# An encoder layer on one core: the start addresses of the moving token tiles, and the order of a chunk's first matmuls

## The chip, the cores and the metric

The kernel runs on one core of one Trainium2 chip. The metric is the device time of one execution in microseconds. Engines are named as the profile names them: PE is the matrix engine, PEld its loading of stationary operands, DVE the vector engine, ACT the scalar engine, POOL GpSimd and SP the engine whose queue issues the weight loads.

## The reference

One layer works on 256 tokens of 2048 channels in float32. Cut to what matters here (`h` is the normalised input):

```python
z = h @ w_in                                   # 2048 -> 13312 columns
conv_b, conv_c, conv_in, q, k, v, g_a, g_b = split(z)
y_a = (conv_b * conv3(conv_c * conv_in)) @ w_out_conv
y_b = block_gqa(rope(rmsnorm(q)), rope(rmsnorm(k)), v) @ w_out_attn
mixed = (sigmoid(g_a + ba) * y_a + sigmoid(g_b + bb) * y_b) @ w_merge
x = x + rmsnorm(mixed, norm_mix_post)
f = square(relu(rmsnorm(x, norm_mlp_pre) @ w_up)) @ w_down
x = x + rmsnorm(f, norm_mlp_post)
```

## The kernel before

All products are done in chunks of 512 weight columns over a contraction of 2048, cut into 16 tiles of 128. Every operand is split into a high part and a low remainder (`split`), so that one product takes three matmuls: high by high, high by low, low by high. Weights come as granules of two contraction tiles: a 128x1024 transfer into `raw`, a cast on ACT into `whi` and a subtraction on DVE into `wlo`.

A chunk is computed in one of two functions.

- `linear_channels` (lines 182, 186 and 189) keeps the weights stationary, 128 columns at a time, and streams the 256 tokens past them. For each granule a loop over the four groups of 128 output channels (`c`) calls `step(c, ...)`, which does both contraction tiles of the granule, three matmuls each. A call therefore has 4 x 16 x 3 = 192 matmuls of 256 columns. The last two granules are done pair by pair of channel groups.
- `linear` (lines 152 to 154) keeps the tokens stationary and streams 512 weight columns past them: 2 x 16 x 3 = 96 matmuls of 512 columns.

In the order of the program: three `linear` calls on `hT` for K, V and the first Q; then, for each of four heads' groups, three `linear_channels` calls on `hT` for the convolution branch with the attention of the group between them (transposes on lines 231 and 419, scores and values on lines 386 to 388), and a `linear` call on `hT` for the next Q; then 16 `linear_channels` calls for gates and branch outputs (`hT` and `yT` by turns, then `hT` and `oT`); four `linear` calls on `mT` for the merge; one `linear` and three `linear_channels` calls on `x2T` for the first quarter of the MLP's up projection; four `linear` calls on `fT` (down projection); and three times four `linear_channels` calls on `x2T` and four `linear` calls on `fT`. `later` and `tick` put the attention's steps at fixed places between the granules, so the order on PE is written out by hand.

The token operands live in three large buffers with the tags A, B and C (`pair`). `LATE` shifts a buffer's data by some floats. What counts below is an **offset**: the start of the moving operand less the start of the stationary one in the same partition, modulo 256 bytes. In the built program all `raw`, `whi` and `wlo` tiles begin at 192 modulo 256. `hT` (tag A, 48 floats late), `yT`, `oT` and `x2T` begin at 128, `mT` and `fT` at 192, K and V (`kv`) at 128, queries and probabilities (`qh`, `ql`, `ph`, `pl`) at 192. Each contraction tile, each half of tokens and each group of channels is a multiple of 256 bytes long, so an operand's offset is the same in all its matmuls:

- `linear_channels`: 128 - 192, which is -64 (192 modulo 256)
- `linear` on `hT` and `x2T`: 192 - 128 = +64
- `linear` on `mT` and `fT`: 0
- scores -64, values +64

Of the kernel before, what the change touches and what calls it, by code (L numbers as in the profile page):

```python
# [9 lines left out]
F32 = mybir.dt.float32  # L10
F32R = mybir.dt.float32r
# [4 lines left out]
P = 128  # L16
D = 2048
T = 256
NT = T // P
KT = D // P  # L20
CH = 512
# [11 lines left out]
def trunk_kernel(  # L33
# [27 lines left out]
    const = ctx.enter_context(tc.tile_pool(name="const", bufs=1))  # L61

    sm = ctx.enter_context(tc.tile_pool(name="sm", bufs=2))
    wts = ctx.enter_context(tc.tile_pool(name="wts", bufs=WB))
    big = ctx.enter_context(tc.tile_pool(name="big", bufs=1))
    wk = ctx.enter_context(tc.tile_pool(name="wk", bufs=2))
    ps_acc = ctx.enter_context(tc.tile_pool(name="ps_acc", bufs=4, space=bass.MemoryType.PSUM))
# [17 lines left out]

    LATE = {"A": {True: 48, False: 0}, "B": {True: 0, False: 16}, "C": {True: 0}}

    def pair(tag, moving):

        n, at = 2 * KT * T, LATE[tag][moving]  # L90
        flat = big.tile([P, n + max(LATE[tag].values())], F32R, tag=tag, name=tag)
        both = flat[:, at : at + n].rearrange("p (h k t) -> p h k t", h=2, k=KT)
        return both[:, 0], both[:, 1]

# [7 lines left out]
    def later(delay, fn):  # L102
        todo.append((clock[0] + 2 * delay, fn))
# [36 lines left out]
    def linear(act, wv, done, k0=0, k1=KT, lag=0, ahead=None):  # L140

        ah, al = act
        accs = [ps_acc.tile([P, CH], F32, name="acc") for _ in range(NT)]

        def step(t, k, wh, wl):
            ts_ = slice(t * P, (t + 1) * P)
            for g in range(KG):
                a = k - k0 + g  # L150
                first, last = a == 0, a == k1 - k0 - 1
                nc.tensor.matmul(accs[t], lhsT=ah[:, a, ts_], rhs=wh[:, g, :], start=first, stop=False)  # L152
                nc.tensor.matmul(accs[t], lhsT=ah[:, a, ts_], rhs=wl[:, g, :], start=False, stop=False)  # L153
                nc.tensor.matmul(accs[t], lhsT=al[:, a, ts_], rhs=wh[:, g, :], start=False, stop=last)  # L154
# [12 lines left out]

    def linear_channels(act, wv, done):

        ah, al = act
        accs = [ps_acc.tile([P, 2, T], F32, name="acc") for _ in range(CH // P // 2)]

        def step(c, k, wh, wl):
            cs = slice(c * P, (c + 1) * P)
            acc = accs[c // 2][:, c % 2, :]
            for g in range(KG):
                a = k + g  # L180

                nc.tensor.matmul(  # L182
                    acc, lhsT=wh[:, g, cs], rhs=ah[:, a, :], start=a == 0 and c % 2 == 0, stop=False,
                    skip_group_check=True,
                )
                nc.tensor.matmul(  # L186
                    acc, lhsT=wh[:, g, cs], rhs=al[:, a, :], start=False, stop=False, skip_group_check=True
                )
                nc.tensor.matmul(  # L189
                    acc, lhsT=wl[:, g, cs], rhs=ah[:, a, :], start=False, stop=a == KT - 1, skip_group_check=True  # L190
                )
# [85 lines left out]

    hT = pair("A", True)

    def first_operands(k, n):  # L280
        xt = mx.tile([P, KA, T], F32, tag="rope", bufs=4, name="xt")
        nc.sync.dma_start(xt[:, :n, :], xT[:, k : k + n, :])
        for i in range(n):
            split(xt[:, i, :], hT[0][:, k + i, :], hT[1][:, k + i, :], scale=g_pre[:, k + i : k + i + 1])

# [95 lines left out]

    oT = pair("C", True)
    yT = pair("B", True)

# [5 lines left out]
    def attention(j):  # L390
# [41 lines left out]
        def heads_out(hp, ovs):  # L432
            h0 = j * GRP + hp
            split(ovs[0], oT[0][:, h0 : h0 + 2, :], oT[1][:, h0 : h0 + 2, :])

# [11 lines left out]
    def conv(j):  # L447
# [29 lines left out]
        def outer(c, acc):  # L477
            b = wk.tile([P, 2, T], F32, tag="cc", bufs=CCB, name="cc")
            with tc.high_priority():
                nc.vector.tensor_tensor(b, acc, cv[:, c : c + 2, :], op=ALU.mult)  # L480
            d = j * 4 + c
            later(2 + c // 2, lambda: split(b, yT[0][:, d : d + 2, :], yT[1][:, d : d + 2, :]))

# [32 lines left out]
    for j in range(4):  # L516
# [6 lines left out]
        linear_channels(yT, w_oc[j], done)  # L523
    mT = pair("B", False)
    for j in range(4):
        g = gate(C_GB, j, 1)
        def done(c, acc):
            y = wk.tile([P, 2, T], F32, tag="cc", bufs=CCB, name="cc")
            with tc.high_priority():
                nc.vector.tensor_tensor(y, acc, g[:, c : c + 2, :], op=ALU.mult)  # L530
            d = j * 4 + c
            nc.vector.tensor_tensor(y, y, m[:, d : d + 2, :], op=ALU.add)
            split(y, mT[0][:, d : d + 2, :], mT[1][:, d : d + 2, :])

        linear_channels(oT, w_oa[j], done)
# [16 lines left out]
    ss1 = ss01[:, 1]  # L552
    ss2 = const.tile([P, NT, 4], F32, name="ss2")
# [20 lines left out]
    def residual(t, x2):  # L574
        r = row_rsqrt(ss1, t, t)
        ts_ = slice(t * P, (t + 1) * P)
        for c in range(4):
# [9 lines left out]
            nc.vector.tensor_tensor(n, tr, g_mlp[:, ds].unsqueeze(2).broadcast_to([P, 4, P]), op=ALU.mult)  # L587
            split(n, x2T[0][:, ds, ts_], x2T[1][:, ds, ts_])

# [15 lines left out]
    facc = big.tile([P, 2, NT, D], F32, tag="B", name="facc")[:, 0]  # L605
    ss3 = const.tile([P, NT, 4], F32, name="ss3")
    outv = out.rearrange("(t p) d -> p t d", p=P)

    def hidden_channels(q, j, fT):


        def done(c, acc):
# [4 lines left out]
            d = j * 4 + c  # L617
            split(f, fT[0][:, d : d + 2, :], fT[1][:, d : d + 2, :])

        linear_channels(x2T, w_up[q * 4 + j], done)  # L620

    def hidden(q, j, fT):
# [9 lines left out]
        def sink(c, tr):  # L632
            d = j * 4 + c
            split(tr, fT[0][:, d : d + 2, :], fT[1][:, d : d + 2, :])

# [43 lines left out]
    for q in range(4):  # L679
        fT = pair("A", False)  # L680
        for j in range(4):
# [67 lines left out]
```

## Time and profile before

| | |
|---|---|
| median of 3 runs | 1602.23 us (1602.12 to 1602.23) |
| the profiled execution | 1602.84 us, span 1601.1 us |
| granted PE clock, mean | 0.999 |
| PE busy | 1589.0 us, 99% of the span |
| PEld busy | 1482.2 us |
| DVE busy, ACT busy | 947.5 us, 710.7 us |
| read from HBM | 302.44 MB, 190 GB/s over the span |

Every line of the profile that speaks of time in the program counts from the first instruction (the span). The profiled execution took 1.7 us more than its span, and 0.6 us more than the median of the runs. PE's busy time is of little use for single matmuls: the profile models a matmul's end, and matmuls overlap. How fast they follow each other is read as the length of a stretch over the number of matmuls that the loops put into it; a stretch's own count also takes in the one or two matmuls still draining at its start.

### The profile page before, as it was taken

The numbers are of one execution on the slowest core, as the hardware profiler recorded it, in microseconds if no ns is written. First come the engines' busy times: TensorE is split into PE (matmuls) and PEld (weight loads), VectorE is DVE, ScalarE is ACT, GpSimd is POOL, SyncE is SP. The second block draws the span as 40 slices with busy tenths as digits, with TensorE's granted clock in tenths as the row PEclk, the third lists the DMA queues.
The fourth block names the chain that finished last, engine by engine and source line by source line (L and its number), as shares of the span: only waits on it lengthen the run. The fifth ranks groups of instructions, "written<-read, shape, count | busy, mean of one in ns | idle before, by whom it ended". The sixth has DMA issues, their size and how long they took to land.

```text
span 1601.1 us, 26865 instructions
## 1 busy us (share of the span) xinstructions
PE 1589.0 (99%) x11210; PEld 1482.2 (93%) x11210; DVE 947.5 (59%) x1107; ACT 710.7 (44%) x860; POOL 35.6 (2%) x23
## 2 busy tenths in 40 slices
PE   9999999999999999999999999999999999999997
PEld 7899999999999999999988898899988998899986
DVE  6767676677765455555555865445655555555654
ACT  7444444444454444444444644434433343333441
POOL 0110101001000000000000000000000000000000
PEclk9999999999999999999999999999999999999999
DMA  8655545555476655666764665655555555556562
GB/s 324 200 176 165 184 148 186 183 174 183 159 248 193 193 192 189 201 195 195 251 206 150 216 192 190 195 188 186 191 191 194 185 189 192 194 184 191 189 206 84
DMA packets 86297, 306.28 MB, mean 191 GB/s; under 512 B 9632, under 2 KB 10016, under 8 KB 85920
## 3 DMA queue, kind: packets, MB, share of 16 engines
q1 hardware_dynamic: 84608, 300.32, 57.8%
q10 hardware_dynamic: 1568, 4.25, 0.8%
q8 instruction: 87, 1.43, 0.4%
q14 instruction: 34, 0.28, 0.1%
HBM read 302.44 MB, written 2.10 MB: 190 GB/s over the span
## 4 chain that ended last, share of the span: by engine, by line
PE 98%; DVE 1%; DMA 0%; POOL 0%; issue 0%; ACT 0%; SPq 0%; DVEq 0%; POOLq 0%; ACTq 0%
PE acc L182 20%; PE acc L186 20%; PE acc L189 20%; PE acc L153 12%; PE acc L154 12%; PE acc L152 12%; PE at L388 0%; PE at L387 0%; PE at L386 0%; PE tr L419 0%; DMA raw<-in_w_in 0%; PE tr L231 0%; POOL rs L243 0%; DVE wlo L77 0%; PE tr L584 0%
## 5 line engine op out<-in xcount | busy, mean ns | idle before, releaser
L77 DVE TENSOR_TENSOR wlo<-raw,whi 128x1024 fp32r<-128x1024 f32 (+1 forms) x561 | 684.3, 1222 | 578.2 <-ACT whi L76 576.3
L76 ACT CAST whi<-raw 128x1024 fp32r<-128x1024 f32 (+1 forms) x561 | 588.5, 1050 | 751.7 <-PE acc L186 380.3
L182 PE MATMUL acc<-A,whi 128*128 128x256 f32 x1280 | 357.2, 279 | 0.0
L189 PE MATMUL acc<-A,wlo 128*128 128x256 f32 x1280 | 355.2, 277 | 0.0
L186 PE MATMUL acc<-A,whi 128*128 128x256 f32 x1280 | 355.2, 277 | 0.0
L182 PE MATMUL acc<-C,whi 128*128 128x256 f32 x1216 | 340.5, 280 | 0.0
L189 PE MATMUL acc<-C,wlo 128*128 128x256 f32 x1216 | 340.3, 280 | 0.0
L186 PE MATMUL acc<-C,whi 128*128 128x256 f32 x1216 | 340.3, 280 | 0.0
L153 PE MATMUL acc<-wlo,A 128*128 128x512 f32 x704 | 275.0, 391 | 1.0 <-DVE wlo L77 1.0
L152 PE MATMUL acc<-whi,A 128*128 128x512 f32 x704 | 274.4, 391 | 1.2 <-ACT whi L76 1.2
L154 PE MATMUL acc<-whi,A 128*128 128x512 f32 x704 | 274.8, 390 | 0.0
L182 PEld LDWEIGHTS acc<-A,whi 128*128 128x128 f32 x1280 | 241.6, 189 | 0.2
L186 PEld LDWEIGHTS acc<-A,whi 128*128 128x128 f32 x1280 | 240.4, 188 | 0.2
L189 PEld LDWEIGHTS acc<-A,wlo 128*128 128x128 f32 x1280 | 240.4, 188 | 0.0
L189 PEld LDWEIGHTS acc<-C,wlo 128*128 128x128 f32 x1216 | 231.5, 190 | 0.0
L182 PEld LDWEIGHTS acc<-C,whi 128*128 128x128 f32 x1216 | 229.0, 188 | 0.2
L186 PEld LDWEIGHTS acc<-C,whi 128*128 128x128 f32 x1216 | 228.2, 188 | 0.2
L153 PEld LDWEIGHTS acc<-wlo,A 128*128 128x128 f32 x704 | 132.3, 188 | 30.3 <-DVE wlo L77 2.6
L152 PEld LDWEIGHTS acc<-whi,A 128*128 128x128 f32 x704 | 132.2, 188 | 29.6 <-ACT whi L76 2.1
L154 PEld LDWEIGHTS acc<-whi,A 128*128 128x128 f32 x704 | 132.3, 188 | 27.4
L182 PE MATMUL acc<-B,whi 128*128 128x256 f32 x256 | 70.7, 276 | 0.0
L186 PE MATMUL acc<-B,whi 128*128 128x256 f32 x256 | 70.7, 276 | 0.0
(144 smaller groups left out, 1112.7 us busy)
## 6 DMA issues: line engine op xcount, KB each, us to landing
raw<-in_w_in SPq DMA_DIRECT2D x207, 512.0 KB, 4.4
raw<-in_w_up SPq DMA_DIRECT2D x128, 512.0 KB, 3.8
raw<-in_w_dn SPq DMA_DIRECT2D x128, 512.0 KB, 3.4
raw<-in_w_oc SPq DMA_DIRECT2D x32, 512.0 KB, 4.4
raw<-in_w_oa SPq DMA_DIRECT2D x32, 512.0 KB, 4.3
raw<-in_w_mg SPq DMA_DIRECT2D x32, 512.0 KB, 4.3
xj<-in_x SPq DMA_DIRECT2D x4, 512.0 KB, 8.3
xr<-in_x ACTq DMA_DIRECT2D x1, 2048.0 KB, 10.0
```

The lines of the kernel that those rows point to most:

```text
L76: nc.scalar.copy(hi, src)
L77: nc.vector.tensor_tensor(lo, src, hi.bitcast(F32), op=ALU.subtract)
L152: nc.tensor.matmul(accs[t], lhsT=ah[:, a, ts_], rhs=wh[:, g, :], start=first, stop=False)
L153: nc.tensor.matmul(accs[t], lhsT=ah[:, a, ts_], rhs=wl[:, g, :], start=False, stop=False)
L154: nc.tensor.matmul(accs[t], lhsT=al[:, a, ts_], rhs=wh[:, g, :], start=False, stop=last)
L182: nc.tensor.matmul(acc, lhsT=wh[:, g, cs], rhs=ah[:, a, :], start=a == 0 and c % 2 == 0, stop=False, skip_group_check=True,)
L186: nc.tensor.matmul(acc, lhsT=wh[:, g, cs], rhs=al[:, a, :], start=False, stop=False, skip_group_check=True)
L189: nc.tensor.matmul(acc, lhsT=wl[:, g, cs], rhs=ah[:, a, :], start=False, stop=a == KT - 1, skip_group_check=True)
```

## The change

Tag A's buffer now holds `hT` as two pieces: its first contraction tile, high and low, at the start of the buffer, and the other fifteen behind it, 16 floats (64 bytes) on. Tag C's buffer holds `oT` and `x2T` the other way round, with the first contraction tile behind the rest. `yT` keeps its tiles together, 64 bytes on. `mT` and `fT` begin at the buffer's start as before. The pool of small tiles is taken after the large ones, which moves the addresses a little, and two small tiles of sums are shared instead of new.

In the built program the weights still begin at 192 modulo 256. The first tile of `hT`, `oT` and `x2T` begins at 192 too, the other fifteen and all of `yT` at 0, `mT` and `fT` at 192, `kv` at 192. So the offsets become:

- `linear_channels` on `hT`, `oT`, `x2T`: 0 in the first contraction tile, +64 in the other fifteen; on `yT`: +64 in all
- `linear` on `hT` and `x2T`: 0 in the first tile, -64 in the other fifteen
- `linear` on `mT` and `fT`: 0 as before
- scores and values: 0

In `linear_channels` the first granule's loops are turned: the first contraction tile is done for all four channel groups, then the second. `fill` splits a block that holds the first tile in two, one piece for each place.

```diff
-    def pair(tag, moving):
-        n, at = 2 * KT * T, LATE[tag][moving]
-        flat = big.tile([P, n + max(LATE[tag].values())], F32R, tag=tag, name=tag)
...
+    GAP = 16
...
+        def __init__(self, tag, moving=False, first=False, last=False):
+            n = 2 * KT * T
+            pad = 3 * GAP if last else GAP
+            flat = big.tile([P, n + pad], F32R, tag=tag, name=tag)
+            self.first = None
+            if first or last:
+                at, rest = (0, 2 * T + GAP) if first else (n - 2 * T + pad, 0)
+                self.first = flat[:, at : at + 2 * T].rearrange("p (h k t) -> p h k t", h=2, k=1)
+                n -= 2 * T
+            else:
+                rest = GAP if moving else 0
+            self.rest = flat[:, rest : rest + n].rearrange("p (h k t) -> p h k t", h=2, k=n // (2 * T))
...
+        def fill(self, k, src, ts_=slice(None)):
+
+            for at, n, hi, lo in self.parts(k, src.shape[1], ts_):
+                split(src[:, at : at + n, :], hi, lo)
...
-                for c in range(CH // P):
-                    step(c, *gran)
+
+                for gs in [[g] for g in range(KG)] if gran[0] == 0 else [range(KG)]:
+                    for c in range(CH // P):
+                        step(c, *gran, gs)
...
-    hT = pair("A", True)
+    hT = Operand("A", first=True)
+    oT = Operand("C", last=True)
...
-    yT = pair("B", True)
+    yT = Operand("B", moving=True)
...
-    mT = pair("B", False)
+    mT = Operand("B")
...
-    x2T = pair("C", True)
+    x2T = Operand("C", last=True)
...
-        fT = pair("A", False)
+        fT = Operand("A")
```

On PE, in the first granule of an up call (`x2T` is C, and the call's two accumulators `acc` hold two channel groups each), these rows of before are the second contraction tile of the second channel group and the first of the third:

```order
L182 MATMUL acc_11145<-C_8882,whi_11149 128x256
L186 MATMUL acc_11145<-C_8882,whi_11149 128x256
L189 MATMUL acc_11145<-C_8882,wlo_11150 128x256
L182 MATMUL acc_11146<-C_8882,whi_11149 128x256
L186 MATMUL acc_11146<-C_8882,whi_11149 128x256
L189 MATMUL acc_11146<-C_8882,wlo_11150 128x256
```

After the change the fourth to fifteenth matmul of the same call are these; the first nine of the rows are the first tile of groups 2, 3 and 4, the last three the second tile of group 1.

```order
L213 MATMUL acc_11149<-C_8883,whi_11153 128x256
L217 MATMUL acc_11149<-C_8883,whi_11153 128x256
L220 MATMUL acc_11149<-C_8883,wlo_11154 128x256
L213 MATMUL acc_11150<-C_8883,whi_11153 128x256
L217 MATMUL acc_11150<-C_8883,whi_11153 128x256
L220 MATMUL acc_11150<-C_8883,wlo_11154 128x256
L213 MATMUL acc_11150<-C_8883,whi_11153 128x256
L217 MATMUL acc_11150<-C_8883,whi_11153 128x256
L220 MATMUL acc_11150<-C_8883,wlo_11154 128x256
L213 MATMUL acc_11149<-C_8883,whi_11153 128x256
L217 MATMUL acc_11149<-C_8883,whi_11153 128x256
L220 MATMUL acc_11149<-C_8883,wlo_11154 128x256
```

The second accumulator is now first written after six matmuls of the call instead of twelve; the number of matmuls and the weights they read are the same. All 12 matmuls of offset 0 stand together at the call's start.

On ACT, while the merge's result is turned into `x2T` (`cc` holds four contraction tiles of it), before:

```order
L76 CAST whi_9646<-raw_9644 128x1024
L76 CAST C_8882<-cc_9478 128x4x128
L76 CAST C_8882<-cc_9488 128x4x128
L76 CAST whi_9664<-raw_9662 128x1024
L76 CAST C_8882<-cc_9498 128x4x128
```

and after:

```order
L75 CAST whi_9650<-raw_9648 128x1024
L75 CAST C_8883<-cc_9479 128x128
L75 CAST C_8883<-cc_9479 128x3x128
L75 CAST C_8883<-cc_9491 128x4x128
L75 CAST whi_9668<-raw_9666 128x1024
L75 CAST C_8883<-cc_9501 128x4x128
```

The cast of the block that holds the first tile has become two. DVE's subtraction is split likewise. This happens three times in the program: once for `oT` and once for each half of the tokens of `x2T`.

## Rows read from the trace of the kernel before

**Rows 1.** The page: busy time, share and instructions by engine.
```profile
PE 1589.0 (99%) x11210; PEld 1482.2 (93%) x11210; DVE 947.5 (59%) x1107; ACT 710.7 (44%) x860; POOL 35.6 (2%) x23
```

**Rows 2.** All waits of PE: us in total, times, longest us.
```profile
PE acc L152 <- ACT whi L76: 1.2, 2, 0.8
PE tr L263 <- DVE half L270: 1.1, 1, 1.1
PE acc L153 <- DVE wlo L77: 1.0, 2, 0.5
PE tr L584 <- DVE mg L579: 0.4, 1, 0.4
```

**Rows 3.** Stages: us; busy (count) PE PEld DVE ACT POOL; clock, DMA share, GB/s.
```profile
76.91:442.09 365.18, 365.18 (x2882) 353.35 (x2881) 254.27 (x374) 171.24 (x238) 22.55 (x8) 1.00 0.54 173
442.09:790.19 348.10, 348.10 (x3074) 348.10 (x3073) 189.17 (x179) 157.08 (x173) 0.00 (x0) 1.00 0.64 207
904.49:972.94 68.45, 68.45 (x586) 68.44 (x584) 42.47 (x45) 30.87 (x34) 0.00 (x0) 1.00 0.66 216
972.94:1060.02 87.08, 87.08 (x386) 72.08 (x385) 42.44 (x37) 38.23 (x41) 0.00 (x0) 1.00 0.60 193
1060.02:1150.48 90.46, 90.46 (x770) 90.45 (x768) 50.41 (x52) 37.09 (x40) 0.00 (x0) 1.00 0.59 187
```

**Rows 4.** PE groups by form, 442.09 to 790.19 us: busy us, mean ns of one.
```profile
L182 PE MATMUL acc<-A,whi 128*128 128x256 f32 x512 | 141.3, 276 | 0.0
...
L182 PE MATMUL acc<-C,whi 128*128 128x256 f32 x256 | 70.7, 276 | 0.0
```

**Rows 5.** PE groups by form, 1060.02 to 1150.48 us.
```profile
L182 PE MATMUL acc<-C,whi 128*128 128x256 f32 x256 | 71.9, 281 | 0.0
```

**Rows 6.** PE groups by form, 76.91 to 442.09 us.
```profile
L189 PE MATMUL acc<-A,wlo 128*128 128x256 f32 x768 | 213.9, 278 | 0.0
...
L387 PE MATMUL at<-kv,qh 128*128 128x256 f32 x32 | 9.0, 281 | 0.0
```

**Rows 7.** PE groups by form, 99.82 to 112.53 us.
```profile
L186 PE MATMUL acc<-A,whi 128*128 128x256 f32 x33 | 9.3, 281 | 0.0
```

**Rows 8.** PE's timeline, four transposes: start us, us, engine, line, names, count.
```profile
93.72 0.60 PE L231 MATMUL tr<-ident,ra 128*128 128x128 f32 x4
```

**Rows 9.** PE groups by form, 91.68 to 93.71 us.
```profile
L182 PE MATMUL acc<-A,whi 128*128 128x256 f32 x6 | 1.7, 276 | 0.0
```

**Rows 10.** PE groups by form, 94.28 to 99.80 us.
```profile
L186 PE MATMUL acc<-A,whi 128*128 128x256 f32 x16 | 4.5, 281 | 0.0
```

**Rows 11.** Single stretches: us, PE busy (count), clock, DMA share, GB/s.
```profile
904.49:909.95 5.46, 5.46 (x49) 1.00 0.93 287
972.94:975.02 2.08, 2.08 (x11) 1.00 0.09 14
994.74:1016.49 21.75, 21.75 (x97) 1.00 0.59 194
248.49:270.47 21.98, 21.98 (x99) 1.00 0.62 192
30.43:36.03 5.60, 5.60 (x26) 1.00 1.01 398
```

**Rows 12.** Values, PE groups by form, 115.72 to 116.25 us.
```profile
L386 PE MATMUL at<-ph,kv 128*128 128x256 f32 x2 | 0.6, 277 | 0.0
```

**Rows 13.** Values, PE groups by form, 119.7 to 120.3 us.
```profile
L386 PE MATMUL at<-ph,kv 128*128 128x256 f32 x2 | 0.6, 280 | 0.0
```

**Rows 14.** The page: the weights' split on DVE and ACT.
```profile
L77 DVE TENSOR_TENSOR wlo<-raw,whi 128x1024 fp32r<-128x1024 f32 (+1 forms) x561 | 684.3, 1222 | 578.2 <-ACT whi L76 576.3
L76 ACT CAST whi<-raw 128x1024 fp32r<-128x1024 f32 (+1 forms) x561 | 588.5, 1050 | 751.7 <-PE acc L186 380.3
```

**Rows 15.** Groups of ACT and of DVE, 880 to 905 us: the split of `x2T`.
```profile
L76 ACT CAST C<-cc 128x512 fp32r<-128x512 f32 x5 | 3.0, 619 | 4.3 <-DVE cc L587 4.3
L77 DVE TENSOR_TENSOR C<-cc,C 128x512 fp32r<-128x512 f32 x5 | 3.3, 685 | 0.0
```

More of the change, by code (lines that the diff above doesn't have):

```diff
@@ L82, in split, with __call__, parts @@
             )
-    LATE = {"A": {True: 48, False: 0}, "B": {True: 0, False: 16}, "C": {True: 0}}
-    def pair(tag, moving):
-        n, at = 2 * KT * T, LATE[tag][moving]
-        flat = big.tile([P, n + max(LATE[tag].values())], F32R, tag=tag, name=tag)
-        both = flat[:, at : at + n].rearrange("p (h k t) -> p h k t", h=2, k=KT)
-        return both[:, 0], both[:, 1]
+    GAP = 16
+    class Operand:
+        def __init__(self, tag, moving=False, first=False, last=False):
[10 more added lines that the diff above has]
+            self.rest = flat[:, rest : rest + n].rearrange("p (h k t) -> p h k t", h=2, k=n // (2 * T))
+        def __call__(self, k, ts_=slice(None)):
+            _, _, hi, lo = self.parts(k, 1, ts_)[0]
+            return hi[:, 0, :], lo[:, 0, :]
+        def parts(self, k, n, ts_=slice(None)):
+            if self.first is None:
+                return [(0, n, self.rest[:, 0, k : k + n, ts_], self.rest[:, 1, k : k + n, ts_])]
+            out = []
+            if k == 0:
+                out.append((0, 1, self.first[:, 0, :, ts_], self.first[:, 1, :, ts_]))
+            lo = max(k, 1)
+            if k + n > lo:
+                ks = slice(lo - 1, k + n - 1)
+                out.append((lo - k, k + n - lo, self.rest[:, 0, ks, ts_], self.rest[:, 1, ks, ts_]))
+            return out
+        def fill(self, k, src, ts_=slice(None)):
+            for at, n, hi, lo in self.parts(k, src.shape[1], ts_):
+                split(src[:, at : at + n, :], hi, lo)
     todo = []
@@ L151, in step @@
                 first, last = a == 0, a == k1 - k0 - 1
-                nc.tensor.matmul(accs[t], lhsT=ah[:, a, ts_], rhs=wh[:, g, :], start=first, stop=False)
-                nc.tensor.matmul(accs[t], lhsT=ah[:, a, ts_], rhs=wl[:, g, :], start=False, stop=False)
-                nc.tensor.matmul(accs[t], lhsT=al[:, a, ts_], rhs=wh[:, g, :], start=False, stop=last)
+                ah, al = act(a, ts_)
+                nc.tensor.matmul(accs[t], lhsT=ah, rhs=wh[:, g, :], start=first, stop=False)
+                nc.tensor.matmul(accs[t], lhsT=ah, rhs=wl[:, g, :], start=False, stop=False)
+                nc.tensor.matmul(accs[t], lhsT=al, rhs=wh[:, g, :], start=False, stop=last)
             if k + KG == k1:
@@ L168, in linear_channels, with step @@
     def linear_channels(act, wv, done):
-        ah, al = act
         accs = [ps_acc.tile([P, 2, T], F32, name="acc") for _ in range(CH // P // 2)]
-        def step(c, k, wh, wl):
+        def step(c, k, wh, wl, gs=range(KG)):
             cs = slice(c * P, (c + 1) * P)
             acc = accs[c // 2][:, c % 2, :]
-            for g in range(KG):
+            for g in gs:
                 a = k + g
+                ah, al = act(a)
                 nc.tensor.matmul(
-                    acc, lhsT=wh[:, g, cs], rhs=ah[:, a, :], start=a == 0 and c % 2 == 0, stop=False,
+                    acc, lhsT=wh[:, g, cs], rhs=ah, start=a == 0 and c % 2 == 0, stop=False,
                     skip_group_check=True,
@@ L283, in first_operands @@
         for i in range(n):
[L284 removed]
+            split(xt[:, i, :], *hT(k + i), scale=g_pre[:, k + i : k + i + 1])
     norm_row = wk.tile([P, 2, T], F32, name="bias", bufs=1)
@@ L433, in heads_out @@
             h0 = j * GRP + hp
-            split(ovs[0], oT[0][:, h0 : h0 + 2, :], oT[1][:, h0 : h0 + 2, :])
+            oT.fill(h0, ovs[0])
         at = 9
@@ L481, in outer @@
             d = j * 4 + c
-            later(2 + c // 2, lambda: split(b, yT[0][:, d : d + 2, :], yT[1][:, d : d + 2, :]))
+            later(2 + c // 2, lambda: yT.fill(d, b))
         linear_channels(hT, w_in[C_CC + j], first)
@@ L532, in done @@
             nc.vector.tensor_tensor(y, y, m[:, d : d + 2, :], op=ALU.add)
-            split(y, mT[0][:, d : d + 2, :], mT[1][:, d : d + 2, :])
+            mT.fill(d, y)
         linear_channels(oT, w_oa[j], done)
@@ L587, in residual @@
             nc.vector.tensor_tensor(n, tr, g_mlp[:, ds].unsqueeze(2).broadcast_to([P, 4, P]), op=ALU.mult)
-            split(n, x2T[0][:, ds, ts_], x2T[1][:, ds, ts_])
+            x2T.fill(c * 4, n, ts_)
     for j in range(4):
@@ L605, in trunk_kernel @@
     facc = big.tile([P, 2, NT, D], F32, tag="B", name="facc")[:, 0]
-    ss3 = const.tile([P, NT, 4], F32, name="ss3")
+    ss3 = ss01[:, 1]
     outv = out.rearrange("(t p) d -> p t d", p=P)
@@ L617, in done @@
             d = j * 4 + c
-            split(f, fT[0][:, d : d + 2, :], fT[1][:, d : d + 2, :])
+            fT.fill(d, f)
         linear_channels(x2T, w_up[q * 4 + j], done)
@@ L633, in sink @@
             d = j * 4 + c
-            split(tr, fT[0][:, d : d + 2, :], fT[1][:, d : d + 2, :])
+            fT.fill(d, tr)
         linear(x2T, w_up[q * 4 + j], done, lag=LAG if q == 0 and j == 0 else 0)
```

10 lines of the change are left out of this document (4 added, 6 removed).

## The prediction, made before the changed kernel ran

> **What bounds the kernel now.** I read the page first: PE is busy for 1589.0 of the 1601.1 us, DVE for 59% and ACT for 44% [rows 1]. The list of PE's waits is nearly empty: 3.7 us in all, none over 1.1 us [rows 2]. So the time is the number of matmuls times the distance between them, and I cut the span into stages at the first matmul of each [rows 3]. The loops say how many matmuls a stage has, and the quotient is the distance. The gate and branch stage has 16 calls of 192: 348.10 us / 3072 = 113.31 ns. An up stage of the MLP has 4 calls of 192: 90.46 us / 768 = 117.79 ns (two more up stages are 90.46 us as well). Same form, same granted clock of 1.00, that is the upper of the clock's two levels, 2.4 GHz; 4.47 ns of difference.
>
> The groups by form say the same without counting. In the gate stage a channel matmul lasts 276 ns in the mean, whichever buffer its tokens come from [rows 4]; in the up stage it lasts 281 ns [rows 5]. Tag C stands in both, at the same address with the same offset of -64 to the same weight buffers. So at this offset there are **two levels that each hold themselves**, and what went before decides between them. I call them fast (276 ns long, 113.31 apart) and slow (281 and 117.79).
>
> What tips them? Inside a call, four transposes do [rows 8]: 276 ns ahead of them [rows 9], 281 behind them and to the call's end [rows 10]. Slow is then handed on: the next call stays slow for its first 96 matmuls [rows 7]. At a call's start it depends on the chunk before. Behind `linear` at offset +64 the first up call ran 48 matmuls in 5.46 us, fast [rows 11]. Behind `linear` at offset 0 the up stages are slow throughout [rows 3, 5]. `linear` has levels of its own: at offset 0 96 matmuls take 21.75 us, 226.6 ns each, exactly twice the fast distance; at +64 they take 229.0 ns in a Q call (21.98 us) and 233.3 ns in the V call (24 in 5.60 us) [rows 11].
>
> The attention stage is mixed: 278 ns in the mean [rows 6], two fifths of the way from 276 to 281, so about 40% of its 2304 channel matmuls are slow.
>
> **The change, part by part.** It removes no matmul and adds none. Each term is a number of matmuls times a distance.
>
> Up projection. If each call begins fast and stays so, three stages give 3 x 768 x 4.47 ns = 10.3 us. In the first quarter the 48 fast matmuls leave 528, at 117.79 ns 62.2 of the 63.0 us that follow (the rest is eight transposes); they give 528 x 4.47 = 2.4 us. Together **-12.7 us**.
>
> Attention. The transposes inside calls stay, and will tip the level again. What a fresh start of each call can take away is slowness handed on: 96 matmuls in each of four head groups [rows 7], 384 x 4.47 = **-1.7 us**. Bounds: -4.1 us if none is slow any more (40% of 2304), +6.2 us if all are.
>
> Scores and values go to offset 0. The 96 score matmuls last 281 ns now [rows 6]; the 96 values 277 behind a fast call and 280 behind a slow one [rows 12, 13]. Between nothing and 0.6 us is to be had; I take half, **-0.3 us**.
>
> The first tile at offset 0. 39 calls have it (20 on `hT`, 4 on `oT`, 15 on `x2T`), 468 matmuls. No channel matmul of before runs at offset 0. The nearest row is `linear` at offset 0, which costs nothing over its fast distance [rows 11]; from above I bound it by `linear`'s worst, 6.7 ns, thus 3.1 us. I take **+1.0 us**, near the lower end, for two changes of offset in every call.
>
> `linear` on `hT` and `x2T` at -64. No `linear` of before runs there. Between 226.6 and 233.3 ns per matmul it is worth from -2.0 us (V and first Q from 233.3, three Q calls from 229.0, all to 226.6) to +1.7 us (those three Q calls and the call on `x2T` from 229.0 to 233.3). I take **0**: the distance of 64 bytes stays and only its sign turns.
>
> The split pieces. Splitting a block in two costs ACT 2 x 619 - 1050 = 188 ns and DVE 2 x 685 - 1222 = 148 ns [rows 14, 15]. One of the three is hidden under the attention stage, where DVE is busy for 254 of 365 us [rows 3]. Two stand where `x2T` is made, the one place where PE waits for DVE's work on it [rows 2]: at most 2 x 0.34 = 0.7 us, and I take **+0.3 us**. Turning the first granule's loops is free: the second accumulator is wanted 0.7 us earlier (6 x 113 ns), and the four buffers give it a whole call's lead.
>
> A faster up stage also needs its weights sooner. The gate stage already lives at that pace, with DMA at a share of 0.64 and DVE at 189 of 348 us [rows 3], so nothing new gets late.
>
> Sum: -12.7 - 1.7 - 0.3 + 1.0 + 0 + 0.3 = -13.4 us. The profiled execution took 1602.84 us, 1.7 more than its span, and comes to 1589.4. It stood 0.6 us above the median of the runs, so I forecast **1588.8 us**.
>
> **The step that no row proves** is that +64 holds the fast level when it is entered from twelve matmuls at 0. For it: values at +64 stay at 277 behind a fast call [rows 12], so +64 has a fast level for 256 columns. Offset 0 never shows another level than the fast one in `linear`. Against it: going from 0 to -64 ends slow every time, and `linear` at +64 never reaches 226.6 ns.
>
> The Trainium skill speaks against the whole change: TensorE: Matmul & The Clock Gate, section "Step-by-step: what each phase is for", says that PE has two independent SBUF read ports and that loading the next stationary tile takes no read bandwidth from the running matmul. By that rule an offset could not matter. The trace has two rates for one form at one clock, so matmuls do depend on something beyond form and clock, though these rows do not prove that it is the address.
>
> **The rivals.**
>
> *+64 holds the slow level.* Then from the thirteenth matmul of a call everything is slow: the gate stage loses 3072 x 4.47 = 13.7 us, attention 6.2, the first up call 0.2, and with 1.0 and 0.3 it is +21.4 us, 1623.6 us; if only the calls on some buffers go that way, from about 1606 on. For it: going from 0 to -64 does just that [rows 5]. Against: the values [rows 12]. It is decided by the distance of matmuls 13 to 24 of a gate call.
>
> *The offset does not matter, or +64 has a middle level.* If only the order of events sets the level, up stays slow and gates fast: 1602.5 us. That is also what the two read ports of the rule above would give. If +64 costs 2.2 ns per matmul (half the gap, as `linear` at +64 lies between its ends), up gains 6.4 us, gates lose 6.8 and 1.3 comes on top: 1603.9 us. Both are no change that a measurement of this kernel can tell, for which I take 0.2%, 3.2 us either way.
>
> *Up goes fast, attention gets worse.* The transposes tip more calls to slow, say 80% in place of 40% (+4.1), and `linear` at -64 takes 233.3 ns (+1.7): 1602.2 - 12.7 + 4.1 + 1.7 + 1.3 = 1596.6 us.
>
> **How the numbers follow.** I give the forecast 0.49, the last rival 0.13, the middle one 0.14 and the first 0.24. The forecast's own range is 1584.5 to 1593 us, from its bounds without all ends falling on one side. Faster by over 0.2% takes the forecast and the last rival: 0.62; within 0.2%: 0.14; slower: 0.24. To leave out no more than 2 in 10, the range runs from 1584.5 to 1614 us: it drops 0.04 below and the dearer half of the slow case.
>
> **What would show it.** Right: an up stage of 87.0 us with matmuls of 276 ns, the gate stage still at 348 us, the attention stage some 2 us shorter, Q calls within 0.5 us of 22. Wrong: 281 ns in the gate stage, an up stage at 90 us, or first tiles slower than the rest by more than 7 ns a matmul. A PE wait for `C` over 1 us near 890 us would show the split pieces mis-sized.

## The result, and the profile after

The changed kernel is slower: 1626.22 us (1625.15 to 1627.09, 4 runs) against 1602.17 us (1600.44 to 1602.23, 4 runs) of the kernel before, a ratio of 1.0152 with an interval of 1.0135 to 1.017. The forecast was 1588.8 us, the range ended at 1614. What came is the first rival, "+64 holds the slow level", which was worked out to 1623.6 us. The profiled execution took 1625.51 us, its span 1623.6 us.

The page's first row of the changed kernel, busy time by engine, answers to [rows 1]:

```profile
PE 1611.3 (99%) x11210; PEld 1502.1 (93%) x11210; DVE 947.9 (58%) x1110; ACT 710.0 (44%) x863; POOL 35.7 (2%) x23
```

PE has the same 11210 instructions and is busy 22.3 us longer; DVE and ACT each have three instructions more, the split pieces, and the same busy time within 0.7 us. All waits of PE, as in [rows 2]:

```profile
PE acc L183 <- ACT whi L75: 1.6, 1, 1.6
PE tr L296 <- DVE half L303: 1.1, 1, 1.1
PE acc L184 <- DVE wlo L76: 0.8, 2, 0.5
PE tr L617 <- DVE mg L612: 0.4, 1, 0.4
```

That is 3.9 us in place of 3.7, and none of it is for `C`. So nothing new waits, and the loss is in the distance of the matmuls. The windows by stage (columns as in [rows 3]): the attention stage, the gate and branch stage, the first up quarter and an up stage; then, inside the gate stage, the first 12 matmuls of a call on `hT`, its other 180, and the call on `yT` behind it; at the end a Q call.

```profile
77.72:449.39 371.67, 371.67 (x2881) 358.36 (x2880) 254.37 (x375) 171.25 (x239) 22.55 (x8) 1.00 0.54 170
449.39:811.61 362.22, 362.22 (x3075) 362.22 (x3074) 189.32 (x179) 156.80 (x173) 0.00 (x0) 1.00 0.63 199
926.15:994.95 68.80, 68.80 (x585) 68.79 (x584) 41.30 (x44) 29.80 (x33) 0.00 (x0) 1.00 0.67 207
1082.03:1172.60 90.57, 90.57 (x769) 90.57 (x768) 50.41 (x52) 37.11 (x40) 0.00 (x0) 1.00 0.61 187
494.65:496.09 1.44, 1.44 (x14) 1.44 (x13) 1.44 (x2) 1.06 (x1) 0.00 (x0) 1.00 0.03 14
496.10:517.29 21.19, 21.19 (x182) 21.19 (x181) 9.31 (x10) 8.13 (x9) 0.00 (x0) 1.00 0.66 199
517.30:539.91 22.61, 22.61 (x194) 22.61 (x193) 11.20 (x11) 9.30 (x10) 0.00 (x0) 1.00 0.58 185
153.85:176.24 22.39, 22.39 (x98) 17.96 (x97) 12.24 (x12) 9.70 (x10) 0.00 (x0) 1.00 0.62 190
```

The granted clock is 1.00 in every one, as before. The gate stage lost 14.1 us (362.22 for 348.10), the attention stage 6.5 (371.67 for 365.18), and the up stage, which was to gain 3.4, took 90.57 us for 90.46. The start, the merge with the first up chunk, and the up stages add 0.8, 0.2 and 0.7: together 22.3 of the 22.5 us by which the span grew. Inside a gate call the first 12 matmuls stand 1.44 us / 12 = 120 ns apart, the 180 that follow 21.19 / 180 = 117.7 ns; the call on `yT`, 22.61 / 192 = 117.8 ns, has the slow level from its first matmul on. The groups by form of the gate stage agree; 280 stands where [rows 4] has 276 (279 in the groups of lines 217 and 220):

```profile
L213 PE MATMUL acc<-A,whi 128*128 128x256 f32 x512 | 143.5, 280 | 0.0
...
L213 PE MATMUL acc<-C,whi 128*128 128x256 f32 x256 | 71.7, 280 | 0.0
L213 PE MATMUL acc<-B,whi 128*128 128x256 f32 x256 | 71.7, 280 | 0.0
```

So the change did not bring the up stages to the level of the gates; it brought the gates to the level of the up stages.

### The profile page after: what moved, and what is told of

The parts are those of the page before. It is cut to its first block, busy times and chain, and to the rows that moved or that the text cites. A ratio compares the mean times of both kernels' runs of the same rounds, so it can differ in the third digit from the quotient of the medians.

```text
span 1623.6 us, 26872 instructions
## 1 busy us (share of the span) xinstructions
PE 1611.3 (99%) x11210; PEld 1502.1 (93%) x11210; DVE 947.9 (58%) x1110; ACT 710.0 (44%) x863; POOL 35.7 (2%) x23
## 4 chain that ended last, share of the span: by engine, by line
PE 98%; DVE 1%; DMA 0%; POOL 0%; issue 0%; ACT 0%; SPq 0%; DVEq 0%; POOLq 0%; ACTq 0%
PE acc L213 20%; PE acc L220 20%; PE acc L217 20%; PE acc L184 12%; PE acc L185 12%; PE acc L183 12%; PE at L419 0%; PE at L421 0%; PE at L420 0%; PE tr L452 0%; DMA raw<-in_w_in 0%; PE tr L264 0%; POOL rs L276 0%; DVE wlo L76 0%; PE tr L617 0%
```

## The experiments

The first question was which part of the change does it: the first tile at offset 0, the rest at +64, or the turned loops. The first theory was that +64 can hold either level and that the twelve matmuls at 0 hand the slow one on, whatever comes behind them. The rivals were that +64 has only the slow level, that the turned loops alone do it, and, later, that the sign of the rest decides. In all fences of this section the rows are windows with the columns of [rows 3].

### All moving tokens at +64, nothing apart

The kernel before, with another table:

```diff
-    LATE = {"A": {True: 48, False: 0}, "B": {True: 0, False: 16}, "C": {True: 0}}
+    LATE = {"A": {True: 16, False: 0}, "B": {True: 0, False: 48}, "C": {True: 0}}
```

> The kernel before with every moving token operand at offset +64 and no first tile apart; linear on mT and fT stays at 0. Theory 1 (the twelve matmuls at offset 0 tip each call to the slow level, and +64 merely keeps the level it is given): the gate stage stays fast, 348 us with matmuls of 276 ns, and the whole is within 8 us of 1602. Rival (the slow level is the only one that +64 has over a whole call): 118 ns per channel matmul everywhere, gate stage 362 us, the whole 1622 to 1626 us.

1607.48 us in one run, span 1605.7 us, beside 1602.41 us (1599.8 to 1604.65, 7 runs) of the kernel before on that chip. The windows are the last 92 matmuls ahead of the gate stage, the gate stage, an up stage and a Q call:

```profile
435.71:446.13 10.42, 10.42 (x94) 10.42 (x93) 5.88 (x7) 4.46 (x5) 0.00 (x0) 1.00 0.76 253
446.13:794.30 348.17, 348.17 (x3075) 348.17 (x3074) 189.29 (x179) 157.31 (x173) 0.00 (x0) 1.00 0.65 207
...
1064.58:1155.03 90.45, 90.45 (x769) 90.45 (x768) 50.40 (x52) 37.20 (x40) 0.00 (x0) 1.00 0.61 187
153.04:175.42 22.38, 22.38 (x98) 18.05 (x97) 12.27 (x12) 9.75 (x10) 0.00 (x0) 1.00 0.60 186
```

The gate stage is fast in all its 3072 matmuls at +64: 348.17 us, 113.3 ns each. So +64 has a fast level, and the rival that it knows only the slow one is out. Where did the fast level come from? In the attention stage ahead of it the first channel call of a head group is slow to its end, and the third turns fast behind its transposes; the last of these calls is fast at its end (10.42 us / 92 = 113.3 ns) and hands that level on to the gates. Not everything moves to +64 here: the scores do, since `kv` is their moving operand, but the values, where `kv` is stationary, come to -64. Behind `linear` at offset 0 the up stage is slow, as it is at -64.

### All at 128, and all at 0

```diff
+    LATE = {"A": {True: 32, False: 0}, "B": {True: 0, False: 32}, "C": {True: 0}}
```

and

```diff
+    LATE = {"A": {True: 0, False: 0}, "B": {True: 0, False: 0}, "C": {True: 0}}
...
+        flat = big.tile([P, n + (64 if tag == "B" else 0)], F32R, tag=tag, name=tag)
```

> The kernel before with every moving token operand at offset 128; linear on mT and fT stays at 0. If the distance of two 64-byte steps, the farthest that 256 bytes allow, has no slow level, every channel matmul is 113.3 ns apart, no call is tipped by transposes, and the whole is 1582 to 1588 us. Rival (the level is set by what ran before and no offset is free of it): a mixture as before, 1595 to 1624 us.

1635.06 us (1634.66 to 1636.94, 4 runs), a ratio of 1.0211 with an interval of 1.0194 to 1.0228. Gate stage and up stage:

```profile
451.77:816.31 364.54, 364.54 (x3074) 364.54 (x3073) 189.26 (x179) 157.07 (x173) 0.00 (x0) 1.00 0.63 197
...
1087.10:1179.25 92.15, 92.15 (x769) 92.15 (x768) 50.42 (x52) 37.28 (x40) 0.00 (x0) 1.00 0.60 184
```

The expectation missed: at 128 no call is fast. Its two distances are 118.7 ns (364.54 us / 3072) and 120.0 (92.15 / 768), both worse than the slow level at -64.

> The kernel before with every token operand at offset 0, stationary and moving. If offset 0 itself is the dearest for channel matmuls, as the twelve first ones of a changed call at 120 ns say, all 8256 are 120 ns apart and the whole is about 1637 us. Rival (120 ns was only the price of going from one offset to another): the fast level, 1582 to 1590 us.

1639.42 us in one run, span 1637.6 us, as expected. Gate stage and up stage:

```profile
451.53:820.17 368.64, 368.64 (x3075) 368.64 (x3073) 189.15 (x179) 157.33 (x173) 0.00 (x0) 1.00 0.62 195
...
1091.43:1183.58 92.15, 92.15 (x769) 92.15 (x768) 50.41 (x52) 37.26 (x40) 0.00 (x0) 1.00 0.60 184
```

At 0 there is one level, 368.64 / 3072 = 120.0 ns, whatever went before. This is the same program as before but for addresses, with the same number of instructions in the stage, and the stage takes 20.5 us more. So start addresses alone move the distance of matmuls, which the rows of before did not prove. The prediction had set against this a rule of the Trainium skill, page TensorE: Matmul & The Clock Gate, section "Step-by-step: what each phase is for": PE reads the moving operand and the next weights through two independent SBUF ports. What it took from that rule, that an offset could not matter, does not hold here. Whether the ports get in each other's way is not shown: the weights stand at 192 in all these runs, so the distance to them and the tokens' own address are not told apart. What the run also shows is that the two functions part at offset 0. `linear` has its best distance there, 226.6 ns for 512 columns [rows 11]; `linear_channels` has its worst, 120.0 for 256.

### Only the loops turned

The kernel before with the first granule's loops turned as in the change:

```diff
+                for gs in [[g] for g in range(KG)] if gran[0] == 0 else [range(KG)]:
+                    for c in range(CH // P):
+                        step(c, *gran, gs)
```

> The kernel before with nothing but the first granule's loops turned, all at offset -64. Both theories: no address changes, so no change: 1602 us within 3, the gate stage at 348 us and the later up stages at 90.5 us. If the order of the first twelve matmuls counted by itself, the gate stage would come to 362 us.

1600.68 us in one run, span 1598.9 us. Gate stage, first up quarter, up stage:

```profile
441.99:790.14 348.15, 348.15 (x3074) 348.15 (x3073) 189.19 (x179) 157.49 (x173) 0.00 (x0) 1.00 0.65 207
904.40:970.81 66.41, 66.41 (x586) 66.41 (x584) 42.39 (x45) 30.97 (x34) 0.00 (x0) 1.00 0.71 222
1057.87:1148.31 90.44, 90.44 (x769) 90.44 (x768) 50.38 (x52) 37.27 (x40) 0.00 (x0) 1.00 0.61 187
```

Gates and later up stages stand as before, so the turned loops are not the cause. The first up quarter is 2.0 us shorter than in [rows 3]: the transposes in its first call left PE at the fast level here and at the slow one before, and the two calls behind kept it. In other runs below it fell either way. A gain of that size in one run says nothing of an edit.

### Only the first tile of `hT` apart, the rest at -64

The kernel before, loops turned, the first contraction tile of `hT` set to 0, to +64 or to 128; every other moving operand stays at -64. With 0:

```diff
+        flat = big.tile([P, n + 48], F32R, tag="A", name="A")
+        one = flat[:, 0 : 0 + 2 * T].rearrange("p (h k t) -> p h k t", h=2, k=1)
+        rest = flat[:, 2 * T + 48 :].rearrange("p (h k t) -> p h k t", h=2, k=KT - 1)
...
-    hT = pair("A", True)
+    hT = first_apart()
```

> The kernel before with the first granule's loops turned and only the first tile of hT moved to offset 0; its other fifteen tiles and all of yT, oT and x2T stay at -64. Theory (the twelve matmuls at 0 run 120 ns apart and hand the slow level on, whichever sign the rest has): the gate calls on hT turn slow, and those on yT and oT inherit it, gate stage 362 us, the whole 1616 to 1621 us. Rival (only the sign +64 does it): gate stage within 2 us of 348, the whole about 1601 us.

1599.15 us in one run, span 1597.3 us, beside 1602.69 us (1600.48 to 1604.88, 13 runs) of the kernel before on that chip. The gate stage, the first 12 matmuls of a call on `hT`, its other 180, and an up stage:

```profile
439.79:788.58 348.79, 348.79 (x3074) 348.79 (x3073) 189.34 (x179) 157.00 (x173) 0.00 (x0) 1.00 0.64 206
483.39:484.80 1.41, 1.41 (x14) 1.41 (x13) 1.41 (x2) 1.05 (x1) 0.00 (x0) 1.00 0.00 0
484.81:505.22 20.41, 20.41 (x182) 20.41 (x181) 9.40 (x9) 8.12 (x9) 0.00 (x0) 1.00 0.65 206
...
1056.32:1146.76 90.44, 90.44 (x769) 90.44 (x768) 50.40 (x52) 37.09 (x40) 0.00 (x0) 1.00 0.59 187
```

Behind twelve matmuls at 0 (1.41 / 12 = 118 ns) the 180 at -64 run at 20.41 / 180 = 113.4 ns. In the changed kernel the same twelve had 117.7 ns behind them. With this my first theory fell: matmuls at 0 do not hand on the slow level whatever the rest. Even the second call of a head group, whose first 96 matmuls were slow before [rows 7], is fast from about its fifteenth matmul until the next transposes. The up stages, whose `x2T` has no tile apart here, stay slow.

> As the run with the first tile of hT at 0, but that tile at +64, the rest at -64. Theory (a call's level is set by where its first matmuls stand against the rest; in the kernel before four of eight changes from values at +64 to channels at -64 ended fast): going from +64 to -64 ends fast, the attention stage loses part of its slow calls, the gate stage stays at 348 to 349 us, the whole 1596 to 1601 us. Rival (any change of offset inside a call tips it to slow): gate stage 362 us, the whole about 1617 us.

1603.02 us in one run; the gate stage and the twelve matmuls at +64:

```profile
441.77:790.40 348.63, 348.63 (x3074) 348.63 (x3073) 189.36 (x179) 156.99 (x173) 0.00 (x0) 1.00 0.64 207
485.35:486.76 1.41, 1.41 (x14) 1.41 (x13) 1.41 (x2) 1.05 (x1) 0.00 (x0) 1.00 0.03 12
```

> As the run with the first tile of hT at 0, but that tile at offset 128, the rest at -64. The 240 first matmuls run at about 119 to 120 ns, some 1.5 us. If only coming from 0 ends slow, the gate stage stays at 348 to 350 us and the whole at 1600 to 1604 us; if any change of offset inside a call ends slow, the gate stage is 362 us and the whole about 1618 us.

1599.12 us in one run; the same two windows:

```profile
439.87:788.76 348.89, 348.89 (x3074) 348.89 (x3073) 189.27 (x179) 157.00 (x173) 0.00 (x0) 1.00 0.64 206
483.48:484.90 1.42, 1.42 (x14) 1.42 (x13) 1.42 (x2) 1.06 (x1) 0.00 (x0) 1.00 0.01 3
```

Three different offsets ahead of -64, and in all 24 gate calls on `hT` the rest is fast: the eight first tiles cost the stage only 0.5 to 0.8 us together (348.63 to 348.89 for 348.10). In the attention stage there is one exception among 36 calls. In the run with +64 the very first channel call stayed slow behind its first tile until the transposes, 12.60 us for 107 matmuls, 117.8 ns:

```profile
80.19:92.79 12.60, 12.60 (x109) 12.60 (x108) 11.67 (x19) 4.63 (x5) 5.63 (x2) 1.00 0.46 147
```

So +64 ahead of -64 nearly always ends fast, not always. That run also lies 2 us above what was expected of it, and 3.9 above the run with 0: its attention stage began 1.9 us later (78.78 for 76.86 us), and its first up quarter fell to the slow level (68.44 for 66.40 us).

### Twelve matmuls at +64 ahead of the up stages

If entering -64 from another offset makes it fast, the same might be had from `linear`, and without a tile apart. Here the last two contraction tiles of `fT` lie so that the last 12 matmuls of each down call have offset +64, as all 96 ahead of the first up call have [rows 11]:

```diff
+        main = flat[:, :m].rearrange("p (h k t) -> p h k t", h=2, k=KT - 2)
+        tail = flat[:, m + 48 : n + 48].rearrange("p (h k t) -> p h k t", h=2, k=2)
...
-        fT = pair("A", False)
+        fT = tail_apart()
```

> The kernel before with the last two contraction tiles of fT 64 bytes lower, so that the last twelve matmuls of each linear call of the down projection run at offset +64 and no longer 0; nothing else. Theory (the level of a call is what the matmuls ahead of it leave, and -64 is entered fast from linear at +64 and slow from linear at 0): the three later up stages go from 90.5 to 87.0 us each, the whole is about 1592 us. Rival (up is slow for another reason, x2T's own data or place): 90.5 us as before, the whole 1602 to 1603 us.

1603.04 us (1602.46 to 1604.79, 10 runs), a ratio of 1.0002 with an interval of 0.9992 to 1.0012. The 12 matmuls at +64, and the up stage behind them:

```profile
1056.58:1059.30 2.72, 2.72 (x13) 2.23 (x12) 1.23 (x1) 1.64 (x2) 0.00 (x0) 1.00 0.59 194
1059.31:1149.75 90.44, 90.44 (x769) 90.44 (x768) 50.40 (x52) 37.09 (x40) 0.00 (x0) 1.00 0.59 187
```

No change: these 12 run at 2.72 / 12 = 227 ns, as at 0, and the up stage is slow. Twelve matmuls of `linear` do not do what twelve of `linear_channels` do.

Nor is a whole `linear` call at +64 a sure way in. Up to the end of the merge this program is the kernel before, with the same addresses; yet the first channel call of its attention stage started slow (first row, 119 matmuls, 117.7 ns), where before it started fast (second row, 113.4 ns). In the run with only the loops turned the first up call did the same: 47 matmuls in 5.53 us, 117.7 ns. So the level that -64 takes at a call's start is not set by program and addresses alone; what else decides it is open.

```profile
76.49:90.50 14.01, 14.01 (x120) 14.00 (x119) 13.08 (x21) 5.83 (x6) 5.63 (x2) 1.00 0.48 151
76.91:90.41 13.50, 13.50 (x120) 13.49 (x119) 12.57 (x21) 5.86 (x6) 5.63 (x2) 1.00 0.47 151
```

### The change with the sign of the rest turned

The changed kernel, with the rest of `hT`, `oT` and `x2T` at -64 in place of +64; first tiles at 0, `yT` still at +64:

```diff
-            pad = 3 * GAP if last else GAP
+            pad = 3 * GAP if first else GAP
...
-                at, rest = (0, 2 * T + GAP) if first else (n - 2 * T + pad, 0)
+                at, rest = (0, 2 * T + 3 * GAP) if first else (n - 2 * T + pad, 0)
```

> The changed kernel with one sign turned: the other fifteen tiles of hT, oT and x2T at -64 in place of +64, the first tile still at 0, yT still at +64. Theory (twelve matmuls at 0 followed by -64 end fast, followed by +64 end slow; the three runs with only hT's first tile apart say so for -64): every call on hT, oT and x2T is fast from about its fourteenth matmul on, up stages 87.2 to 87.5 us in place of 90.5, the whole 1586 to 1593 us; the four calls on yT may go either way, 3.4 us between them. Rival (x2T is slow in up for another reason than its entry): up stages 90.5 us, the whole 1598 to 1603 us.

1595.53 us (1595.01 to 1597.21, 6 runs) against 1600.8 us (1600.26 to 1603.11, 10 runs), a ratio of 0.9967 with an interval of 0.9955 to 0.9979. The gate stage, in it a call on `hT` and the call on `yT` behind it, and an up stage:

```profile
441.02:793.60 352.58, 352.58 (x3074) 352.58 (x3073) 189.31 (x179) 156.99 (x173) 0.00 (x0) 1.00 0.63 204
485.47:507.32 21.85, 21.85 (x194) 21.85 (x193) 10.75 (x10) 9.18 (x10) 0.00 (x0) 1.00 0.61 193
507.33:529.93 22.60, 22.60 (x194) 22.60 (x193) 11.21 (x11) 9.36 (x11) 0.00 (x0) 1.00 0.60 187
...
1061.61:1148.97 87.36, 87.36 (x769) 87.36 (x768) 50.35 (x52) 37.18 (x40) 0.00 (x0) 1.00 0.61 193
```

With the sign turned the up stage does what the prediction wanted of it: 87.36 us. The whole lies 2.5 us above the range that was expected of this run. The calls on `yT`, all at +64 behind a fast call at -64, are slow at 22.60 us each.

> The same with the first granule's loops turned back, so that three matmuls at 0 and three at -64 alternate. If only the last change of offset counts, the level is fast behind the first granule as well and the whole is within 2 us of the run with the sign turned. If it takes a longer stretch at the other offset to tip a call, up stages stay at 90.5 us and the whole at 1598 to 1603 us.

The same without the turned loops (`for gs in [range(KG)]`): 1595.21 us in one run. Gate stage and up stage:

```profile
440.24:792.82 352.58, 352.58 (x3074) 352.58 (x3073) 189.27 (x179) 156.97 (x173) 0.00 (x0) 1.00 0.64 204
1061.33:1148.70 87.37, 87.37 (x769) 87.37 (x768) 50.35 (x52) 37.18 (x40) 0.00 (x0) 1.00 0.61 193
```

So the turned loops are not needed. Offsets 0 and -64 then alternate every three matmuls in the first granule, and the call still ends fast.

### +64 entered from other offsets

The mirror image: the rest at +64, the first tile of `hT` at -64 or at 128, the other moving operands and also `mT` at +64 (which makes the merge some 2.3 us dearer). With -64:

```diff
+            pad = 48 if first else 32 if tag == "C" else 0
...
+            if first:
+                at, rest = n - 2 * T + pad, GAP
...
+                rest = 32 if tag == "C" else 0
```

> The changed kernel with the first tile of hT at -64 and its rest at +64, oT, x2T and yT all at +64, and mT at +64 as well, which makes the four merge calls about 2.5 us dearer. Theory of the sign (entering +64 from any other offset inside a call ends slow): gate stage 361 us, the whole 1620 to 1627 us. Rival (it is 0 that must not stand ahead of +64): gate stage 348 to 350 us, the whole 1600 to 1612 us.

1622.71 us in one run, span 1620.9 us. The gate stage, the first 12 matmuls of a call on `hT`, its other 180:

```profile
445.75:807.23 361.48, 361.48 (x3074) 361.48 (x3073) 189.29 (x179) 156.59 (x173) 0.00 (x0) 1.00 0.62 199
490.98:492.34 1.36, 1.36 (x14) 1.36 (x13) 1.36 (x2) 1.05 (x1) 0.00 (x0) 1.00 0.06 24
492.35:513.54 21.19, 21.19 (x182) 21.19 (x181) 9.40 (x10) 8.13 (x9) 0.00 (x0) 1.00 0.61 197
```

This is the sharpest of the runs. The call before, on `yT`, is slow; twelve matmuls at -64 bring PE to the fast level (1.36 / 12 = 113 ns), here and in six more of the eight gate calls on `hT`; and the 180 at +64 behind them fall back at once to 117.7.

> As the run before, with the first tile of hT at 128 and the rest at +64. Theory of the sign: gate stage 361 us, the whole 1620 to 1627 us. Rival (only 0 ahead of +64 ends slow): gate stage 348 to 351 us, the whole 1600 to 1612 us.

1623.48 us in one run, gate stage:

```profile
446.16:808.02 361.86, 361.86 (x3074) 361.86 (x3073) 189.36 (x179) 156.77 (x173) 0.00 (x0) 1.00 0.62 199
```

The same from 128. Counted over every call with a tile apart, up to the next transposes: matmuls at +64 that are entered from 0, -64 or 128 inside a call go slow in all 79 calls of the changed kernel and these two runs; matmuls at -64 that are entered from 0, +64 or 128 go fast in 176 of 177 calls of the three runs with the first tile of `hT` apart, the two with the turned sign and the run that follows.

### `yT` at -64 as well

What was open then: the turned sign gave 1595.5 us, 7 more than the forecast, and some 3 of these lie in the four calls on `yT`. This run takes the version with the turned sign and without the turned loops, and moves `yT` alone (two small tiles share a place, so that all other addresses stand):

```diff
+            pad = 3 * GAP if first or tag == "B" else GAP
...
-                rest = GAP if moving else 0
+                rest = 3 * GAP if moving else 0
```

> Kernel: the turned-sign version without the turned loops, and besides the four calls on yT at -64 in place of +64 (no first tile apart; they begin right behind a fast call on hT). The computation is whole. If a level is handed on from channel call to channel call where the sign stays -64, all four yT calls are fast: 21.7 us each in place of 22.50, so 1595.2 - 4 x 0.78 = 1592.1 us (1591 to 1593.5). Rival: the yT calls were slow for another reason (their storage, or their coming behind a gate) and stay at 22.5: 1595.2 us. Second rival: yT falls to slow by itself and hands the slow level on to oT, whose first tile brings it back: 1595.2 with oT's first dozen matmuls as now.

1593.37 us (1591.66 to 1593.85, 5 runs) against 1602.67 us (1600.67 to 1604.85, 9 runs), a ratio of 0.9937 with an interval of 0.9923 to 0.995: the best version, ahead of both kernels. The attention stage, the gate stage, a call on `yT`, the first up quarter and an up stage:

```profile
78.18:441.74 363.56, 363.56 (x2881) 351.65 (x2880) 254.28 (x375) 171.16 (x239) 22.54 (x8) 1.00 0.54 174
441.75:790.86 349.11, 349.11 (x3074) 349.11 (x3073) 189.27 (x179) 157.04 (x173) 0.00 (x0) 1.00 0.63 206
...
507.19:528.94 21.75, 21.75 (x194) 21.75 (x193) 11.15 (x11) 9.37 (x11) 0.00 (x0) 1.00 0.59 194
905.35:972.40 67.05, 67.05 (x585) 67.05 (x584) 41.36 (x44) 29.89 (x33) 0.00 (x0) 1.00 0.65 213
1059.47:1146.83 87.36, 87.36 (x769) 87.36 (x768) 50.35 (x52) 37.18 (x40) 0.00 (x0) 1.00 0.61 193
```

The `yT` calls took 21.75 us in place of 22.60, so it was their offset. The gate stage gave back 3.5 us; of that the median shows 2 (1593.37 for 1595.21 to 1595.53 us), since in the profiled execution the first up quarter fell slower here (67.05 for 66.46 us in the run of the turned sign with the turned loops) and the start took 0.9 us longer (the attention stage began at 78.18 for 77.24). Beside the kernel before as it ran at the same time, the gain is 9.3 us here and was 5.3 there.

## Why the prediction was wrong, point by point

**The bound and the two levels: right.** PE's distance sets the time in every run, with some 4 us of waits. That there are two levels which hold themselves is shown in both directions: at +64 by the gates of the first experiment, at -64 by the gates and up stages before. What it said of tipping was too simple: four transposes can also turn a slow call fast, as in the first up call with only the loops turned, and a call at -64 behind `linear` at +64 can start at either level (117.7 ns with the turned loops, 113.8 before [rows 11]).

**The step that failed is the one named as such: "that +64 holds the fast level when it is entered from twelve matmuls at 0".** +64 holds a level, but from 0 it takes the slow one; in the changed kernel that happens in every call, and `yT`, which has no tile apart, keeps it. That the offset of the twelve is not at fault is shown by the same twelve ahead of -64, which end fast, and that the side on which the rest stands is, by twelve fast matmuls at -64 ahead of +64, which end slow. Of the evidence weighed there, the argument against ("going from 0 to -64 ends slow every time") was about `linear` at 0 ahead of `linear_channels`, and does not carry over to a step inside a call. The argument for, the values at +64 behind a fast call [rows 12], misled: calls on `yT` at +64 behind a fast call at -64 are slow from their first matmul. The values are six matmuls of another pair of buffers, with `kv` stationary and `ph` moving; why they looked fast is open.

**Up projection, forecast -12.7: nothing came.** The price of a level was right, and so was the place: with the sign turned an up stage took 87.36 us, 3.1 less than before. The missing 0.3 us to the forecast of 87.0 are the four first tiles.

**Gates, forecast 0: +14.1 us.** The first rival's 3072 x 4.47 ns = 13.7 us, plus eight calls on `hT` and four on `oT` with their first tiles.

**Attention, forecast -1.7, bounds -4.1 to +6.2: +6.5 us.** The bound for "all slow" was 6.2. Behind some of the transposes a few matmuls are still fast, so its channel matmuls lost less than that, about 4.7 us; three Q calls and the scores and values, below, add 1.8 us to the stage. The gain that was forecast is there with the sign turned: 363.56 us in the last run, 1.6 less than before.

**Scores and values, forecast -0.3: a loss.** The groups of the attention stage show 283 to 285 ns for scores at 0 in place of 281, and 282 to 283 for values in place of 277 to 279; 192 matmuls by some 3 ns are about 0.6 us. Offset 0 is the worst for 256 columns here too.

**The first tile at 0, forecast +1.0, bounds 0 to 3.1: mis-sized.** 120 ns, 6.7 above the fast distance, over 468 matmuls would be 3.1 us, the upper bound. (Beside the slow level, which the change got, it is 2.2 ns and 1.0 us.) The step took `linear` at 0 as the nearest row [rows 11], and 256 columns with stationary weights have their worst distance there, as the run with all at 0 shows. The best version pays it: a call on `hT` with a tile apart takes 21.83 us, one on `yT` without 21.75.

**`linear` on `hT` and `x2T` at -64, forecast 0, bounds -2.0 to +1.7: near the upper bound.** A Q call took 22.39 us in place of 21.98 [rows 11], three of them 1.2 us. "Only its sign turns" was no argument: the first experiment has the same 22.38.

**Split pieces, forecast +0.3: not seen.** PE has no wait for `C`, and from the merge's start to the end of the first `x2T` chunk the changed kernel took 926.15 - 811.61 = 114.5 us, before 904.49 - 790.19 = 114.3 [rows 3], a difference in which that chunk at -64 is contained.

**The rivals.** The first came true near its price: 1623.6 us worked out, 1626.2 measured. On the span it is +21.4 us worked out beside +22.5. The Q calls (1.2 us), the scores and values (0.6) and the later start (0.8) are not in its sum, and the attention's channel matmuls lost 1.5 less than its 6.2; the other terms fit within a few tenths. The rest of the gap between the medians is scatter: the profiled execution was 0.7 us above the median before and 0.7 below it after. The chance of 0.24 was too low, since the only channel matmuls of before that followed offset 0 had gone slow [rows 5].

**What stays open.** Why -64 goes slow behind whole calls of `linear` at 0 and fast behind twelve matmuls of `linear_channels` at 0: the run with twelve `linear` matmuls at +64 did not separate the number of columns from which operand the weights are. Why one entry of 177 at -64 stayed slow. Whether the difference of the two addresses counts or the tokens' own address modulo 256: no run moved the weights. And no run shows what the two levels are; the sign rule is an observation over these offsets and this weight layout.

## What to carry to other kernels

When a stage of matmuls without waits differs by a few per cent from another of the same form at the same clock, look at the start addresses of both operands; changes of addresses, with three small instructions more in the fastest version, moved this kernel between 1593 and 1639 us. Evidence for a level must come from the same pair of operands, the same number of columns and the same way in: six matmuls of another pair did not tell what 180 would do. A forecast that rests on one unproven step should give the case in which it fails a chance as large as the trace's only like case suggests.

## What the runs showed of the hardware

All at a granted clock of 1.00, the level of 2.4 GHz, and with weights at 192 modulo 256: matmuls of 256 moving columns with stationary weights follow each other at 113.3 or 117.8 ns at offsets of -64 and +64, at 118.7 or 120.0 at 128, and at 120.0 alone at 0. Matmuls of 512 columns with moving weights take 226.7 ns at 0, 229.0 to 233.3 at +64 and up to 233.2 at -64 (a Q call, 22.39 us / 96). At -64, entry from another offset inside a channel call gave 113.3 in 176 of 177 calls; at +64 such an entry gave 117.8 in 79 of 79. Entry into -64 from a whole `linear` call at +64 gave either (113.4 ns before and 117.7 in the run with `fT`'s tail at +64, in the same call at the same addresses), and so do four transposes inside a call.
